# mLSTM start states padded with zero rows per pair of heads, and the low part of the differential queries in both row halves: products over all 128 rows

## The chip, the core and the metric

The kernel runs on one core of one Trainium2 chip. A core has a matrix engine (TensorE, PE in the profile, with its weight loads as PEld), a vector engine (VectorE, DVE), a scalar engine (ScalarE, ACT), GpSimd (POOL) and a synchronisation engine (SyncE, SP) that only issues transfers here. The metric is the device time of one execution in microseconds; 0.5% is 8.5 us.

## The reference, cut to what matters

One inference step of two layers over 640 tokens: 512 latent tokens (tiles 0 to 3 of 128) and 128 context tokens (tile 4). Layer 0 has eight latent-attention heads and four differential heads, layer 1 an mLSTM of eight heads in two directions; a feed-forward block follows each. Two places matter.

A differential head subtracts two attention maps, each with 64 features:

```python
k1, k2 = dk_all[..., :DIFF_HD], dk_all[..., DIFF_HD:]      # DIFF_HD = 64
p = softmax_probs(q1, k1, scale_b) - lam * softmax_probs(q2, k2, scale_b)
out = jnp.einsum('bhqk,bhkd->bhqd', p, dv_all)
```

An mLSTM head computes, per chunk of tokens and direction, a sum of two products: weighted scores times values, and queries times the state before the chunk (64 x 128, with a normaliser as column 129):

```python
s = jnp.einsum('bhcld,bhcsd->bhcls', qc, kc) * jnp.exp(dlog - m_t[..., None])
inter = jnp.exp(m_inter - m_t)
num = jnp.einsum('bhcls,bhcse->bhcle', s, vc) + inter[..., None] * jnp.einsum('bhcld,bhcde->bhcle', qc, Cp)
den = jnp.sum(s, axis=-1) + inter * jnp.einsum('bhcld,bhcd->bhcl', qc, np_)
```

## The kernel before

Activations stay in the core's memory; weights are streamed. SyncE loads a weight tile `wr` (L170) into a ring of four buffers, ScalarE rounds it to a high part `whi` (L180) and VectorE subtracts to get the low part `wlo` (L181). A product with weights is three products: high by high, high by low, low by high (L275 to L277, L295). The same ring of four also holds differential query stacks `qst`, mLSTM keys by token `kn` and, in layer 1, the tiles `state`. The instructions of an engine run in the order of its program; an engine that waits holds up all that is behind it.

*Differential heads* (about 262 to 340 us). `q_stack(t, p)` makes the queries of token tile t for a pair of heads: for each of two maps ScalarE writes the high part into both row halves (L897, L898), and GpSimd writes the low part (L899) into the 64 rows of that map only, both maps into the same 128 columns. The keys `kst` hold a map's high part in one row half and its low part in the other. A map's score (L947, L948) is then a product over 128 rows with the high queries (512 latent columns, then 128 cached ones), and a second over 64 rows with the low queries. Maximum and exponential (VectorE L859, ScalarE L864), combination, transposes (L873) and value products (L975) follow, in a software pipeline in which other items' products stand between.

*The mLSTM loop* (about 1057 to 1163 us) takes ten steps. A table, `HEAD_STEP`, sets the order of the parts in a step and which head each is for; the heads overlap, so that the outputs of one head run beside the scores of the next. Heads come in pairs: the even one has its 64 features in rows 0 to 63, the odd one in rows 64 to 127 (`rows_of(h)`, short `rr`). The parts that matter:

- `load_pair` (L1284): per pair, the tile `state`, the queries `qp` times a decay (broadcast by SyncE L1288, product on GpSimd L1291).
- `s_mm` (L1363): scores `st`, five products over the 64 rows of the head.
- `s_mul` (L1370, L1372): VectorE multiplies by the decays `D`, GpSimd masks.
- `s_state` (L1394, L1400): six products `cs` give a chunk's contribution; VectorE updates the states before chunks 2 to 4 of both directions, on the head's 64 rows. The state before the first chunk is the given one, `C0n`, loaded once (L1162).
- `last_state` (L1407): products `cst` for the final states of the context tokens.
- `o_mm` (L1422, L1423): for a token tile and a direction, the state product over the head's 64 rows, then the value product over 128 rows into the same sums `ho`. In the rows, `ho<-ph,qp` is a state product with the given state, `ho<-state,qp` one with an updated state.
- `o_post` (L1429 to L1437): ScalarE and VectorE divide by the normaliser and add the two directions; `h_norm` (L1453 to L1461) norms the head.

In steps 6 to 8 the table `LOOP_OUT` puts transposes (`mt`, L397) and first output products (`op`, L275 to L277) between the parts.

Of the kernel before, what the change touches and what calls it, by code (L numbers as in the profile page):

```python
# [17 lines left out]
NT = 5            # token tiles of 128: 0-3 latent (sample), 4 context (prompt)  # L18
# [6 lines left out]
# adaLN dots of later vectors (pairs of half dots), spread over the steps of the phases  # L25
ADA_IN = [0, 0, 0, 2, 2, 2, 2, 2, 1, 1, 1, 0, 0]     # by product of the input projections
ADA_FFN = [0] + [2] * 8 + [1] * 13                   # by feed-forward tile of layer 0
ADA_VO = [1, 0, 1, 1]                                # by column chunk of layer 1's values and output gates
ADA_MLA = {1: 1, 2: 1, 3: 1, 4: 1, 5: 1, 6: 1, 9: 1, 11: 1, 13: 1, 14: 1, 16: 1, 19: 1, 21: 1, 24: 2, 26: 1, 28: 1, 29: 1, 31: 1, 33: 1, 34: 1, 36: 1, 38: 1}     # half dots beside an item of MLA (head * 5 + tile)
# attention pipeline: order of the parts within a step, and how many items behind the newest a part is  # L30
# [4 lines left out]
# key stacks (head, map) beside an item of MLA  # L35
KEY_STACKS = {2: [(0, 0), (0, 1), (1, 0)], 10: [(1, 1)], 11: [(2, 0)], 15: [(2, 1), (3, 0)], 17: [(3, 1)], 16: [(4, 0)], 26: [(4, 1)]}
# transposes of a finished half tile (tile, half) after the differential item (tile, head)
MERGED_T = {(3, 3): [(2, 1), (4, 1)], (2, 2): [(1, 1)], (1, 3): [(0, 0), (0, 1)], (2, 0): [(1, 0)], (3, 2): [(2, 0), (3, 0), (4, 0)]}
# what follows the attention: first halves and rest of the output products, by tile
ATT_END = [('begin', 0), ('begin', 2), ('begin', 1), ('step', 4), ('step', 1), ('begin', 3), ('step', 2), ('T', 3), ('step', 0), ('step', 3)]  # L40
# a step of the mLSTM loop: its parts, and their head's distance from the step
HEAD_STEP = [('last', -2), ('state', -1), ('scores', 0), ('out0', -1), ('keys', 0), ('weights', 0), ('out1', -1), ('out3', -1), ('pair', 1), ('out2', -1), ('out4', -1), ('decay', 1)]
# work of the output projection that is taken into the loop, before a part of a step
LOOP_OUT = {(7, 'scores'): [('begin', 0)], (6, 'out3'): [('T', 2)], (7, 'out1'): [('T', 3)], (8, 'out0'): [('T', 4)], (8, 'weights'): [('begin', 1)], (6, 'keys'): [('T', 0)], (6, 'out4'): [('T', 1)], (8, 'out2'): [('begin', 2)], (8, 'decay'): [('begin', 3)]}
OUT_ORDER = [4, 0, 2, 1, 3]
GROUPS = [(0, 8), (8, 16), (16, 22)]   # feed-forward tiles of 128 by group
# [8 lines left out]
def _build(ctx, tc, nc, A):  # L55
# [6 lines left out]
    sp = pool("sp", 12)  # L62
# [37 lines left out]
    # ------------------------------------------------------------ constants  # L100
# [14 lines left out]
    def sigmoid(out, src):  # L115
        # 1 / (1 + exp(-src)) = exp(-ln(1 + exp(-src)))
        S.activation(out, src, AF.Exp, scale=-1.0)
        S.activation(out, out, AF.Ln, bias=ones[0:out.shape[0]])
        S.activation(out, out, AF.Exp, scale=-1.0)

    # silu(c): columns for the tensor engine, and rows on all partitions for the vector engine
# [9 lines left out]
    # ------------------------------------------------------------ weights: streamed, split in two  # L131
# [63 lines left out]
    def done(n=1, prep=True):  # L195
        # without prep the next weights are loaded, and split by a later call
# [8 lines left out]
    # ------------------------------------------------------------ adaLN  # L205
# [8 lines left out]
    def ada_dot(l, j, m, w, cs_=(0, 1)):  # L214
        # w [128 features, 1024]: products with silu(c), summed along the row
# [57 lines left out]
    # ------------------------------------------------------------ products  # L273
# [5 lines left out]
    def nat(ps, hh, hl, t, ch, part=None):  # L279
        # ps [128 tok, cols] = h[tile t] @ w chunk; a part: only the first or second half of the sum  # L280
# [9 lines left out]
    def trans_gemm(outs, wh, wl, hh, hl, nkc=8):  # L290
        # outs: [(psum ap, column slice)]; psum = w^T @ h^T[:, columns]
# [11 lines left out]
    def start_pair(us, wfs, hh, hl, norm_last):  # L303
        # the first two products after a norm leave the last token tiles for the end: their norm comes last
# [5 lines left out]
    # ------------------------------------------------------------ norms  # L310
# [8 lines left out]
    @contextmanager  # L319
    def after_split():  # L320
        # what the block traces is issued behind the last split
        with tc.issue_after(split_ins[0]), tc.issue_after(split_ins[1]):
            yield
# [7 lines left out]
    def ssq0(x_ap):  # L331
        # mean square of the first half of the columns, plus eps
# [49 lines left out]
    class Halves:  # L382
        # h^T of a mixer's output, high and low part of a column half in one tile
# [119 lines left out]
    o = 0  # L503
# [1152 lines left out]
```

## Time and profile before

| | |
|---|---|
| median of three runs | 1692.18 us (1684.17 to 1692.19) |
| span of the profiled execution | 1689.8 us (its own time is about 2.4 us more) |
| TensorE busy | 1662.4 us, 98% of the span |
| VectorE, ScalarE, GpSimd busy | 975.3 us, 697.5 us, 143.2 us |
| differential heads, 262 to 340 us | TensorE 75.58, VectorE 62.76, ScalarE 66.96, GpSimd 17.85 us |
| mLSTM loop, 1056.6 to 1163 us | TensorE 105.89, VectorE 74.98, ScalarE 56.09, GpSimd 43.02 us |

The shares of the whole span hide the stages: the feed-forward blocks take some 1000 of the 1690 us and are dense products. The two last lines of the table are windows on the two stages that the change touches. A TensorE record's printed length holds the pipeline's fill, so consecutive records overlap; how long one really takes is read from the distance between starts.

### The profile page before, as it was taken

Reading aid. Unit: us, or ns where it says so; the run is one execution under the profiler, and the core shown is the slowest. Engines: PE = TensorE matmul, PEld = TensorE weight load, DVE = VectorE, ACT = ScalarE, POOL = GpSimd, SP = SyncE. Lnnn points to the kernel's source line nnn. Section 1 sums busy time; section 2 is a strip of 40 time slices with the busy share of each in tenths; the row PEclk is TensorE's granted clock in tenths of the full one; section 3 lists DMA queues with packets and bytes.
Section 4 is the critical chain, followed back from the end, with each engine's and each line's share of the span. In section 5 each row is a group of like instructions: output and inputs, shape, how many; then the busy total and the mean of one; then the engine's idle time right before and its main releaser. Section 6 shows DMA issues by size and latency. Waiting matters only on the chain.

```text
span 1689.8 us, 24496 instructions
## 1 busy us (share of the span) xinstructions
PE 1662.4 (98%) x9704; PEld 1495.6 (89%) x9704; DVE 975.3 (58%) x1714; ACT 697.5 (41%) x1462; POOL 143.2 (8%) x171
## 2 busy tenths in 40 slices
PE   8999999999999999999999999999999999999998
PEld 7878888788998899889989979777899989998996
DVE  7788887856665655445475385856643343334335
ACT  5433568836332233223262256644643213322332
POOL 0001101210000000000010015532100000000000
PEclk8999999999999999999999999969999999999999
DMA  9363130052453433233225335323332122213211
GB/s 337 121 198 123 51 101 1 14 177 75 147 174 103 147 125 112 67 108 113 88 100 175 125 120 187 99 63 118 107 115 74 56 92 83 75 51 100 76 38 63
DMA packets 55970, 181.55 MB, mean 107 GB/s; under 512 B 7120, under 2 KB 9936, under 8 KB 55856
## 3 DMA queue, kind: packets, MB, share of 16 engines
q1 hardware_dynamic: 51152, 165.07, 30.5%
q0 software_dynamic: 4560, 14.73, 2.6%
q8 instruction: 76, 1.25, 0.3%
q14 instruction: 38, 0.31, 0.1%
q10 hardware_dynamic: 144, 0.20, 0.0%
HBM read 173.26 MB, written 6.71 MB: 106 GB/s over the span
## 4 chain that ended last, share of the span: by engine, by line
PE 93%; DVE 3%; ACT 3%; DMA 1%; issue 0%; SPq 0%; POOL 0%; DVEq 0%; ACTq 0%
PE ffa L295 18%; PE ffb L295 18%; PE fo L277 6%; PE fo L275 6%; PE fo L276 6%; PE qk L295 3%; PE op L275 2%; PE op L277 2%; PE op L276 2%; PE in L275 2%; PE av L931 2%; PE in L277 2%; PE in L276 2%; PE vo L277 2%; PE s L915 2%; PE vo L276 2%
## 5 line engine op out<-in xcount | busy, mean ns | idle before, releaser
L180 ACT CAST whi<-wr 128x1024 fp32r<-128x1024 f32 (+2 forms) x195 | 200.9, 1033 | 621.9 <-PE ffa L295 210.9
L181 DVE TENSOR_TENSOR wlo<-wr,whi 128x1024 fp32r<-128x1024 f32 (+2 forms) x195 | 236.0, 1214 | 222.6 <-ACT whi L180 221.1
L218 DVE SCALAR_TENSOR_TENSOR junk<-araw,cB 128x1024 bf16<-128x1024 f32 x160 | 195.1, 1247 | 32.3 <-DMA araw<-w_adaT 31.9
L277 PE MATMUL fo<-whi,hl 128*128 128x512 f32 (+1 forms) x446 | 175.6, 394 | 0.0
L275 PE MATMUL fo<-whi,hh 128*128 128x512 f32 (+1 forms) x446 | 174.7, 392 | 0.0
L276 PE MATMUL fo<-wlo,hh 128*128 128x512 f32 (+1 forms) x446 | 173.9, 390 | 0.0
L295 PE MATMUL ffa<-hl,whi 128*128 128x320 f32 (+1 forms) x704 | 164.2, 311 | 0.0
L295 PE MATMUL ffa<-hh,whi 128*128 128x320 f32 (+1 forms) x704 | 163.7, 310 | 0.0
L295 PE MATMUL ffa<-hh,wlo 128*128 128x320 f32 (+1 forms) x704 | 162.8, 309 | 0.0
L295 PE MATMUL ffb<-hl,whi 128*128 128x320 f32 (+1 forms) x704 | 162.1, 308 | 0.7 <-DVE hl L328 0.7
L295 PE MATMUL ffb<-hh,whi 128*128 128x320 f32 (+1 forms) x704 | 162.0, 308 | 0.3 <-ACT hh L327 0.2
L295 PE MATMUL ffb<-hh,wlo 128*128 128x320 f32 (+1 forms) x704 | 160.9, 306 | 0.0
L295 PEld LDWEIGHTS ffb<-hl,whi 128*128 128x128 f32 x704 | 118.2, 187 | 1.1 <-DVE hl L328 1.1
L295 PEld LDWEIGHTS ffb<-hh,whi 128*128 128x128 f32 x704 | 118.1, 188 | 0.9 <-ACT hh L327 0.9
L295 PEld LDWEIGHTS ffb<-hh,wlo 128*128 128x128 f32 x704 | 118.7, 188 | 0.0
L295 PEld LDWEIGHTS ffa<-hh,wlo 128*128 128x128 f32 x704 | 118.7, 188 | 0.0
L295 PEld LDWEIGHTS ffa<-hh,whi 128*128 128x128 f32 x704 | 118.2, 188 | 0.5
L295 PEld LDWEIGHTS ffa<-hl,whi 128*128 128x128 f32 x704 | 118.3, 187 | 0.1
L403 DVE TENSOR_TENSOR tmp<-fo,g 128x512 f32<-128x512 f32 (+1 forms) x61 | 41.6, 681 | 131.8 <-PE fo L277 131.7
L276 PEld LDWEIGHTS fo<-wlo,hh 128*128 128x128 f32 x446 | 83.8, 188 | 19.7
L277 PEld LDWEIGHTS fo<-whi,hl 128*128 128x128 f32 x446 | 83.8, 188 | 18.9
L275 PEld LDWEIGHTS fo<-whi,hh 128*128 128x128 f32 x446 | 83.7, 188 | 18.5
(362 smaller groups left out, 3047.6 us busy)
## 6 DMA issues: line engine op xcount, KB each, us to landing
wr<-ffi SPq DMA_DIRECT2D x88, 512.0 KB, 3.7
araw<-w_adaT SPq DMA_DIRECT2D x80, 512.0 KB, 4.1
wr<-ffo SPq DMA_DIRECT2D x44, 512.0 KB, 3.5
D<-m_dram SPq DMA_DIRECT2D x16, 320.0 KB, 4.2
ada<-w_ada SPq DMA_DIRECT2D x9, 512.0 KB, 9.7
wr<-winvo SPq DMA_DIRECT2D x12, 384.0 KB, 3.3
wr<-w_oab SPq DMA_DIRECT2D x8, 512.0 KB, 4.0
g<-gd POOLq DMA_DIRECT2D x8, 512.0 KB, 6.3
```

The source lines that it names most:

```text
L180: S.copy(hi, raw)
L181: V.tensor_tensor(out=lo, in0=raw, in1=hi.bitcast(F32), op=ALU.subtract)
L218: V.scalar_tensor_tensor(out=junk, in0=w, scalar=1.0, in1=cB[:, c, :], op0=ALU.mult, op1=ALU.mult, accum_out=vecs[l][:, j, m, c:c + 1])
L275: PE.matmul(ps, sh, mh, start=first, stop=False)
L276: PE.matmul(ps, sh, ml, start=False, stop=False)
L277: PE.matmul(ps, sl, mh, start=False, stop=last)
L295: PE.matmul(ps, w_(kc), h_[:, kc, sl], start=(kc == 0 and i == 0), stop=(kc == nkc - 1 and i == 2))
L403: V.tensor_tensor(out=tmp, in0=ps, in1=gate[:, 0 if t < 4 else 1, cols], op=ALU.mult)
L915: PE.matmul(sps[:, p, 0:320], qa[0:96, tok], ka[0:96, p * 320:(p + 1) * 320], start=True, stop=True)
L931: PE.matmul(ops[:, 0:64], st["PT"][:, b * 128:(b + 1) * 128], vhead[h][:, kb + b, :], start=(b == 0), stop=(b == nb - 1))
```

## The change

1. `q_stack` writes the low queries of each map into both row halves, in 128 columns for each map (the tile grows from 384 to 512 columns a head). GpSimd makes four subtractions a stack instead of two. The low score products then contract all 128 rows, as the high ones do.
2. The updated states live in a tile of their own, `stp`, zeroed once by GpSimd at the start, with a slot for each head of a pair; a slot holds the head's state in its 64 rows and zeros in the other head's rows. `o_mm` multiplies all 128 rows of `qp` with such a slot. The number of products, their columns and VectorE's updates (64 rows) stay. The tile `state` no longer takes a buffer of the weight ring.
3. The given states come padded with zero rows from the host (`C0p`): two transfers instead of one at the start of layer 1, and one more, issued by GpSimd, in `load_pair` for the third and fourth pair.
4. To make room: eleven instead of twelve buffers in the pool of small tiles, and a smaller room (4096 bytes) for the descriptors of transfers that GpSimd issues. Comments are stripped, so line numbers shift.

```diff
-    sp = pool("sp", 12)
+    sp = pool("sp", 11)
+    stp = cp.tile([128, 2, 2, 2, 3, 129], F32, name="stp")
+    G.memset(stp.rearrange("p a e d k c -> p (a e d k c)"), 0.0)
...
     def q_stack(t, p):
-        q_ = qst[(t, p)] = Wp.tile([128, 2, 384], F32R, name=nm("qst"), tag="raw", bufs=4)
+        q_ = qst[(t, p)] = Wp.tile([128, 2, 512], F32R, name=nm("qst"), tag="raw", bufs=4)
         for i in range(2):
             src = dqT[own(i), 2 * p:2 * p + 2, t * 128:(t + 1) * 128]
-            S.copy(q_[own(i), :, i * 128:(i + 1) * 128], src)
-            S.copy(q_[other(i), :, i * 128:(i + 1) * 128], src)
-            G.tensor_tensor(out=q_[own(i), :, 256:384], in0=src,
-                            in1=q_[own(i), :, i * 128:(i + 1) * 128].bitcast(F32), op=ALU.subtract)
+            hi = slice(i * 128, (i + 1) * 128)
+            S.copy(q_[own(i), :, hi], src)
+            S.copy(q_[other(i), :, hi], src)
+            for r in (own(i), other(i)):
+                G.tensor_tensor(out=q_[r, :, 256 + i * 128:384 + i * 128], in0=src, in1=q_[own(i), :, hi].bitcast(F32), op=ALU.subtract)
...
-                for w, rr in ((q_[:, i * 128:(i + 1) * 128], slice(0, 128)), (q_[r, 256:384], r)):
-                    PE.matmul(sps[:, 0, :], w, kst[h][rr, i, :], start=(w.shape[0] == 128), stop=(w.shape[0] == 64))
-                    PE.matmul(sps[:, 1, 0:128], w, kst[4][rr, h, i, :], start=(w.shape[0] == 128), stop=(w.shape[0] == 64))
+                for part in range(2):
+                    w = q_[:, part * 256 + i * 128:part * 256 + (i + 1) * 128]
+                    PE.matmul(sps[:, 0, :], w, kst[h][:, i, :], start=(part == 0), stop=(part == 1))
+                    PE.matmul(sps[:, 1, 0:128], w, kst[4][:, h, i, :], start=(part == 0), stop=(part == 1))
...
-    C0n = carve(1032).rearrange("p (d a c) -> p d a c", d=2, c=129)
+    C0p = carve(1032).rearrange("p (a e d c) -> p a e d c", a=2, e=2, c=129)
...
-    G.dma_start(C0n, A["C0n"])
+    for a in range(2):
+        G.dma_start(C0p[:, a], A["C0p"][a])
...
     def load_pair(pr):
-        states[pr] = Wp.tile([128, 2, 3, 129], F32, name=nm("state"), tag="raw", bufs=4)
+        states[pr] = stp[:, pr % 2]
+        if pr > 1:
+            G.dma_start(C0p[:, pr % 2], A["C0p"][pr])
...
     def s_state(h):
-                before = states[pr][rr, d, k - 1, :] if k else C0n[rr, d, pr, :]
-                V.scalar_tensor_tensor(out=states[pr][rr, d, k, :], in0=before, scalar=decs[pr][rr, d, i:i + 1],
+                before = states[pr][rr, h % 2, d, k - 1, :] if k else C0p[rr, pr % 2, h % 2, d, :]
+                V.scalar_tensor_tensor(out=states[pr][rr, h % 2, d, k, :], in0=before, scalar=decs[pr][rr, d, i:i + 1],
...
     def o_mm(h, t):
-                before = states[pr][rr, d, k - 1, :] if k else C0n[rr, d, pr, :]
-                PE.matmul(pv[:, d, :], qp_of(pr, d)[rr, t * 128:(t + 1) * 128], before, start=True, stop=False)
+                before = states[pr][:, h % 2, d, k - 1, :] if k else C0p[:, pr % 2, h % 2, d, :]
+                PE.matmul(pv[:, d, :], qp_of(pr, d)[:, t * 128:(t + 1) * 128], before, start=True, stop=False)
...
-    nc = bacc.Bacc("TRN2", target_bir_lowering=False, num_devices=1)
+    nc = bacc.Bacc("TRN2", target_bir_lowering=False, num_devices=1, dynamic_dma_scratch_size=4096)
```

On TensorE, in the loop, the outputs of one head (its token tiles 0, 3 and 1) before, where `D` are the masked scores and `state`, `ph` the updated and the given state:

```order
L1422 MATMUL ho_10264<-ph_8147,qp_9551 128x129
L1423 MATMUL ho_10264<-v_1640_8682,D_10103 128x129
L1422 MATMUL ho_10284<-state_10057,qp_9551 128x129
L1423 MATMUL ho_10284<-v_1640_8682,D_10103 128x129
L1422 MATMUL ho_10284<-state_10057,qp_9551 128x129
L1423 MATMUL ho_10284<-v_1640_8682,D_10110 128x129
L1422 MATMUL ho_10297<-state_10057,qp_9551 128x129
L1423 MATMUL ho_10297<-v_1640_8682,D_10103 128x129
L1422 MATMUL ho_10264<-state_10057,qp_9551 128x129
L1423 MATMUL ho_10264<-v_1640_8682,D_10110 128x129
```

and after:

```order
L1431 MATMUL ho_10281<-ph_8165,qp_9570 128x129
L1432 MATMUL ho_10281<-v_1640_8701,D_10120 128x129
L1431 MATMUL ho_10301<-stp,qp_9570 128x129
L1432 MATMUL ho_10301<-v_1640_8701,D_10120 128x129
L1431 MATMUL ho_10301<-stp,qp_9570 128x129
L1432 MATMUL ho_10301<-v_1640_8701,D_10127 128x129
L1431 MATMUL ho_10314<-stp,qp_9570 128x129
L1431 MATMUL ho_10281<-stp,qp_9570 128x129
L1432 MATMUL ho_10281<-v_1640_8701,D_10127 128x129
L1432 MATMUL ho_10314<-v_1640_8701,D_10120 128x129
```

The products stand in the same alternation, but for one value product that now comes two places later; what differs is that L1431 reads 128 rows where L1422 read 64, which these rows don't print.

On SyncE, at the end of the loop, the last loads of decays (`D`, of the last heads) and of output weights (`w_oc`) before:

```order
L1305 DMA D_10363<-m_dram 128x640 [waits DMAHW4_49,PE_49,Pool_49]
L170 DMA wr_10507<-w_oc 128x1024 [waits DMAHW5_49,DVE_49]
L1305 DMA D_10493<-m_dram 128x640 [waits DMAHW6_49,PE_49,Pool_49]
L1411 DMA o_C<-co_10373 64x2x128 [waits DMAHW7_49,Activation_49]
L1305 DMA D_10500<-m_dram 128x640 [waits DMAHW0_49,PE_49,Pool_49]
L170 DMA wr_10941<-w_oc 128x1024 [waits DMAHW1_49,DVE_49,PE_49]
L1411 DMA o_C<-co_10516 64x2x128 [waits DMAHW2_49,Activation_49]
L170 DMA wr_10947<-w_oc 128x1024 [waits DMAHW5_49,DMAHW3_49,DVE_49]
```

and after:

```order
L1313 DMA D_10380<-m_dram 128x640 [waits DMAHW4_49,PE_49,Pool_49]
L173 DMA wr_10524<-w_oc 128x1024 [waits DMAHW5_49]
L173 DMA wr_10958<-w_oc 128x1024 [waits DMAHW6_49,DVE_49]
L173 DMA wr_10964<-w_oc 128x1024 [waits DMAHW7_49,Pool_49]
L1419 DMA o_C<-co_10390 64x2x128 [waits DMAHW0_49,Activation_49]
L1313 DMA D_10510<-m_dram 128x640 [waits DMAHW1_49,PE_49]
L1313 DMA D_10517<-m_dram 128x640 [waits DMAHW2_49,PE_49]
```

Two loads of output weights now stand ahead of the last head's decays, one of them behind a wait for GpSimd.

On GpSimd, in the differential heads, two query stacks in a row before:

```order
L899 TENSOR_TENSOR qst_2988<-Sa_662,qst_2988 64x2x128 x2
L899 TENSOR_TENSOR qst_3159<-Sa_662,qst_3159 64x2x128 x2
L992 TENSOR_TENSOR mg_1385<-mg_1385,rq_2852 128x512
L993 TENSOR_TENSOR mg_1385<-mg_1385,ph_135 128x512
L899 TENSOR_TENSOR qst_3266<-Sa_662,qst_3266 64x2x128 x2
```

and after:

```order
L904 TENSOR_TENSOR qst_2996<-Sa_664,qst_2996 64x2x128 x4
L904 TENSOR_TENSOR qst_3169<-Sa_664,qst_3169 64x2x128 x4
L997 TENSOR_TENSOR mg_1387<-mg_1387,rq_2858 128x512
L998 TENSOR_TENSOR mg_1387<-mg_1387,ph_137 128x512
L904 TENSOR_TENSOR qst_3278<-Sa_664,qst_3278 64x2x128 x4
```

Each stack's group has four operations in place of two; the norm of a finished tile (`mg`) stays behind the same stack.

## Rows read from the trace of the kernel before

**Rows 1.** The page: span, busy time of the engines, chain that ended last.

```profile
span 1689.8 us, 24496 instructions
...
PE 1662.4 (98%) x9704; PEld 1495.6 (89%) x9704; DVE 975.3 (58%) x1714; ACT 697.5 (41%) x1462; POOL 143.2 (8%) x171
...
PE 93%; DVE 3%; ACT 3%; DMA 1%; issue 0%; SPq 0%; POOL 0%; DVEq 0%; ACTq 0%
```

**Rows 2.** Time line of TensorE in the loop (start, length, instruction, shape, count).

```profile
1090.90 0.37 PE L1422 MATMUL ho<-ph,qp 64*128 64x129 f32 x1
1091.01 0.27 PE L1363 MATMUL st<-qk 64*128 64x128 f32 x1
...
1091.43 0.49 PE L1423 MATMUL ho<-v,D 128*128 128x129 f32 x2
1091.85 0.49 PE L1422 MATMUL ho<-state,qp 64*128 64x129 f32 x2
1092.27 0.49 PE L1423 MATMUL ho<-v,D 128*128 128x129 f32 x2
...
1093.52 0.71 PE L1422 MATMUL ho<-state,qp 64*128 64x129 f32 x4
1094.16 0.71 PE L1423 MATMUL ho<-v,D 128*128 128x129 f32 x4
```

**Rows 3.** The same time line after the clock has fallen.

```profile
1111.44 2.84 PE L1394 MATMUL cs<-v,ph 128*64 128x129 f32 x12
1114.21 1.22 PE L1363 MATMUL st<-qk 64*128 64x128 f32 x4
...
1120.72 0.80 PE L1422 MATMUL ho<-state,qp 64*128 64x129 f32 x2
1121.45 0.80 PE L1423 MATMUL ho<-v,D 128*128 128x129 f32 x2
```

**Rows 4.** Windows by loop step: stretch, length, busy of each engine (records), clock.

```profile
1067.89:1076.55 8.66, 8.66 (x59) 6.78 (x59) 7.33 (x22) 5.75 (x22) 5.08 (x6) 1.00 0.45 109
1076.55:1087.43 10.88, 10.88 (x68) 8.35 (x67) 10.36 (x35) 7.33 (x31) 7.88 (x10) 1.00 0.33 90
...
1097.31:1111.44 14.13, 13.62 (x69) 10.09 (x68) 11.15 (x34) 8.09 (x34) 8.09 (x11) 0.82 0.39 108
1111.44:1125.94 14.50, 14.50 (x56) 11.36 (x55) 5.59 (x17) 5.71 (x24) 2.06 (x3) 0.50 0.16 51
...
sum 105.12, PE 104.61 PEld 79.74 DVE 74.00 ACT 54.81 POOL 42.99; mean PE 11.62 PEld 8.86 DVE 8.22 ACT 6.09 POOL 4.78
```

**Rows 5.** Time line of TensorE before the fall: idle time and its releaser in brackets.

```profile
1103.52 0.49 PE L1422 MATMUL ho<-state,qp 64*128 64x129 f32 x2 [0.49 <-DVE state L1400]
```

**Rows 6.** Windows of 2 us where the clock falls and where it returns.

```profile
1106.00:1108.00 2.00, 2.00 (x10) 1.66 (x9) 1.18 (x7) 0.95 (x6) 1.58 (x3) 0.56 0.63 248
...
1136.00:1138.00 2.00, 2.00 (x9) 1.65 (x8) 1.49 (x6) 1.44 (x6) 0.00 (x0) 0.76 0.66 242
```

**Rows 7.** Time line of TensorE in the differential heads.

```profile
293.46 0.48 PE L947 MATMUL s<-kst,qst 128*128 128x512 f32 x1
...
293.93 0.49 PE L947 MATMUL s<-kst,qst 64*128 64x512 f32 x1
...
294.42 0.50 PE L947 MATMUL s<-kst,qst 128*128 128x512 f32 x1
...
300.78 0.50 PE L947 MATMUL s<-kst,qst 128*128 128x512 f32 x1
...
301.18 1.12 PE L975 MATMUL av<-Sb,ph 128*128 128x128 f32 x8
```

**Rows 8.** Windows of 20 us, 260 to 340 us: one, and the sum.

```profile
300.00:320.00 20.00, 19.07 (x121) 14.46 (x120) 18.06 (x44) 18.20 (x57) 5.38 (x7) 1.00 0.00 1
...
sum 80.00, PE 77.58 PEld 60.52 DVE 63.68 ACT 68.47 POOL 17.85; mean PE 19.39 PEld 15.13 DVE 15.92 ACT 17.12 POOL 4.46
```

**Rows 9.** Time line of GpSimd: the second subtraction of a query stack.

```profile
286.23 0.73 POOL L899 TENSOR_TENSOR qst<-Sa,qst 64x256 fp32r<-64x256 f32 x1 [1.28 <-ACT qst L897]
```

More of the change, by code (lines that the diff above doesn't have):

```diff
@@ L1414, in o_mm @@
     def o_mm(h, t):
-        pr, rr = h // 2, rows_of(h)
+        pr = h // 2
         po = u1("ho")
@@ L1616, in _layout @@
     C0 = np.concatenate([f("state_mlstm_C")[0, 0], f("state_mlstm_n")[0, 0][..., None]], -1)
-    d["C0n"] = C0.reshape(2, 4, 2, 64, 129).transpose(2, 3, 0, 1, 4).reshape(128, 2, 4, 129)
+    C0 = C0.reshape(2, 4, 2, 64, 129)
+    C0p = np.zeros((4, 2, 64, 2, 2, 129), np.float32)
+    for e in range(2):
+        C0p[:, e, :, e] = C0[:, :, e].transpose(1, 2, 0, 3)
+    d["C0p"] = C0p.reshape(4, 128, 2, 2, 129)
     m0 = f("state_mlstm_m")[0, 0]
```

## The prediction

> **What bounds the kernel now.** I read the page first: the profiled execution has a span of 1689.8 us, TensorE is busy 98% of it and holds 93% of the chain that ended last [rows 1]. The reported times of the three runs are 1692.18, 1684.17 and 1692.19 us; what lies around the span is about 2.4 us (1692.2 less 1689.8), so the profiled execution is one like the median, and I count from 1692.2. A TensorE that is always busy says little by itself, because a busy record may be waiting for its weights. So the second view is the time line of TensorE in the two stages that the change touches: the mLSTM loop (about 1057 to 1163 us) and the differential heads (about 262 to 340 us). What to look for there is the distance from one start to the next, not the printed length of a record.
>
> In the loop, products over 64 rows (state products, L1422) alternate with products over 128 rows (values, L1423). Two records of one shape followed by two of the other take 0.42 us: 1091.43 to 1091.85, and 1091.85 to 1092.27. Four records of one shape take 0.64 us (1093.52 to 1094.16) [rows 2]. Two more of the same shape therefore cost 0.22 us, 0.11 each, and the two that came with a change of shape paid 0.42 less 0.22 = 0.20 us for it. At the lower of the two clock levels the same arithmetic holds: twelve records of one shape take 2.77 us (0.23 each, 1111.44 to 1114.21), an alternating pair 0.73 us (1120.72 to 1121.45), so 0.73 less 0.46 = 0.27 us a change [rows 3].
>
> The third view is the table of the loop by steps, cut at the products of the new states [rows 4]. TensorE fills each step, VectorE is at 7.33 of 8.66 and 10.36 of 10.88 us in two of them, and over 105.12 us VectorE is busy 74.00, ScalarE 54.81, GpSimd 42.99. VectorE is next in line, and close. The fourth is the clock: after a wait of 0.49 us of a state product for VectorE [rows 5], in a step with fewer records for its length than the ones before (69 in 14.13 us against 68 in 10.88) [rows 4], the granted clock goes to the lower level (1.2 GHz) and returns only when the dense products of the output projection run; the 2 us windows show 0.56 at 1106 and 0.76 at 1136, so some 30 us at half clock [rows 6].
>
> **The change part by part.** *State products over 128 rows.* Records and columns stay the same (128 state products); only the row shape changes. From the program order of both kernels I counted neighbours of different shape in the loop's TensorE program: 146 before, 46 after. So 100 changes go, at 0.20 us: 20 us of TensorE's 104.61. That a 128-row record is no dearer than a 64-row one by itself is in [rows 2]: 0.22 us for two of either, once the change is taken off. Without those changes and at full clock (half of 30 us, 15 us, comes back), TensorE would need 104.6 - 20 - 15 = about 70 us. It then isn't the bound: VectorE's 74.00 us are. How full VectorE can be is between its two fullest steps: 95% (10.36 of 10.88) gives 78 us for the loop, 85% (7.33 of 8.66) gives 87 [rows 4]. I take 84, nearer to the second, since VectorE there waits in chains (absolute value, maximum, reciprocal, scale) for ScalarE: 105 - 84 = **21 us saved**, bounds 18 to 27.
>
> The Trainium skill, TensorEngine Tiling (Performance Considerations, When to Use Tiling), speaks against this edit: a contraction of 64 should be run as two row tiles beside each other, not padded. The trace has such pairs, but few: a state product of one head starts at 1090.90 and a score product of the next head, in the other row half, 0.11 us later, within the state product's printed 0.37 us [rows 2]. By that rule alone each of the 64 pairs of state products could halve, 64 x 0.11 = 7 us (an estimate by that page), and the change would give it away; but the program puts no two state products of different halves together.
>
> What is lost of overlap is about two records in each of seven steps: 14 x 0.11 = **1.5 us added** (0 to 4.5, if each of them pays a change, 14 x 0.20, besides) [rows 2].
>
> *Low part of the differential scores over 128 rows.* A map's score is a pair of products (512 and 128 columns) over 128 rows, and a pair over 64. Pair to pair takes 0.47 us (293.46 to 293.93) and 0.49 (to 294.42). The one pair that stands between 128-row neighbours takes 0.40 (300.78 to 301.18) [rows 7]. 64 pairs at 0.08 are 5 us; at the loop's 0.20 a change they would be 13. But here ScalarE is nearly full: 18.20 of 20 us between 300 and 320, 68.47 of 80 over the stage [rows 8]. At 91% throughout the 80 us can't shrink below 75.2. So **4 us saved**, 0 to 5. The clock is 1.00 here throughout and gives nothing back.
>
> *More work on GpSimd.* A query stack takes four subtractions instead of two: 16 more at 0.73 us, 12 us of GpSimd. The last of a stack ends at 286.96 and its first low product starts at 293.93, 7 us later [rows 9, 7]; two more end at 288.4 and still come in time. That cover hides all of it. If VectorE were held up for as long as GpSimd works, it would cost 12 us of a stage in which VectorE is free for 16 of 80 [rows 8]; I count **1 us**, 0 to 4.
>
> *Edits with one answer, nothing:* the zeroing at the start (GpSimd, nothing is queued behind it there but a key load that is used in the differential heads), the start states in two transfers instead of one at the same place, and two more transfers issued by GpSimd in the loop, each a step ahead of its first reader; queued behind each is a masking operation on GpSimd, which is busy 42.99 of 105 us [rows 4]. One buffer less among the small tiles and less room for descriptors show in no wait of the loop. On SyncE's queue the states no longer occupy a buffer of the weight ring, so two loads of output weights move ahead of the last decay load (second piece of order in the section on the change); one of them waits for GpSimd's last reader of the keys. The decay is used a step later, and a step is 8.7 us or more [rows 4], so I add nothing; if that cover goes, it costs one transfer once.
>
> Sum: -21 - 4 + 1.5 + 1 = -22.5 us; 1692.2 - 22.5 = 1669.7, **1670 us**.
>
> **The rivals.** *The clock still falls for some 30 us* (1676). For it: VectorE will make TensorE wait more often than the one 0.49 us of now, and the fall came behind such a wait [rows 5, 6]. Against it: every step gets more records into its time, since the alternation was what stretched them. TensorE then needs 104.6 - 20 = 85 us, with waits about 90, so 15 instead of 21: 1692.2 - 15 - 4 + 2.5 = 1676.
>
> *The clock falls early and stays* (1713): the one that ends slower. If the waits for VectorE bring the lower level already in the second step, and it lasts until the output products, seven of nine steps run at half clock: 70 us x 7/9 = 54, doubled 109, and 18 for the last two, 127 instead of 105: +22 - 4 + 2.5 gives 1712.7. It decides the sign when the time at half clock is over twice the present 30 us (each further us there costs about half of one, and 22 are to be lost). For it speaks that TensorE would have 70 us of work in 84; against it that in the differential heads TensorE waits too (19.07 busy of 20) at a clock of 1.00 [rows 8].
>
> *It doesn't do what it says* (1694): the 0.42 us belong to the alternation of two products that add to one bank, not to the row shape; then only the additions are left, 1692.2 + 2.5 = 1694.7. Against it: in the four-and-four stretch, products into the same banks run at 0.16 each over the four [rows 2], and the pair between 128-row neighbours is quicker [rows 7].
>
> **How the numbers follow.** The forecast (clock holds, VectorE next) has a chance of 0.70, the 30 us fall 0.15, no effect 0.09, early fall 0.06. The forecast's bounds are -27 - 5 = -32 (1660) and -18 + 4.5 + 4 = -9.5 (1683); with the second case (1676) up to 1684 some 8 in 10 is covered: 1660 to 1684. A measurement here can tell 0.5%, 8.5 us, from no change, so faster means under 1683.7: 0.84 (the first two, less a little of their upper tail), same 0.10, slower 0.06.
>
> **What would show it.** Right: state and value products one behind the other at 0.11 us; 0.32 to 0.40 us a pair in the differential scores; a granted clock of 1.00 through the loop; waits of TensorE for VectorE's state updates that are not there now; the loop at 78 to 87 us and the differential stage 0 to 5 us shorter. Wrong: 0.42 us for two and two with all rows alike (the price isn't the shape); a clock of 0.50 in the loop (a rival); waits of the low score products for GpSimd (the cover is gone); or a loop of over 90 us at full clock, in which a chain through VectorE and ScalarE, and not VectorE's sum, sets the step.

## The result

The changed kernel takes 1663.07 us (median of four runs, 1662.57 to 1663.80) against 1692.06 us for the kernel before beside it (1684.17 to 1692.19); the ratio is 0.9856, with a 95% interval from 0.9818 to 0.9894. The profiled execution has a span of 1661.2 us instead of 1689.8. In later runs the kernel before lay between 1676 and 1692 us, with mean clocks over the whole execution from 0.997 to 0.985, and the execution profiled before the prediction was one at the slow end.

The page of the changed kernel, lines answering to [rows 1]:

```profile
span 1661.2 us, 24515 instructions
...
PE 1627.4 (98%) x9704; PEld 1483.4 (89%) x9704; DVE 975.0 (59%) x1714; ACT 693.5 (42%) x1462; POOL 162.2 (10%) x191
...
PE 90%; DVE 5%; ACT 3%; DMA 1%; issue 1%; POOL 0%; SPq 0%; DVEq 0%; ACTq 0%
```

TensorE has 35 us less of busy time, as many records as before, and VectorE's share of the chain has grown from 3% to 5%. The landmarks of the time line (first differential score, first output product, first score product of the loop, last value product) split the 28.6 us: 1.7 before the differential heads (the mean clock up to there was 0.97 and is 0.98), 4.3 in them (73.7 to 69.4 us), 23.0 in the loop (107.2 to 84.2), and 0.4 given back elsewhere.

The time line of TensorE in the loop, to set beside [rows 2] (start, length, instruction, shape, count):

```profile
1055.55 0.39 PE L1431 MATMUL ho<-stp,qp 128*128 128x129 f32 x2
1055.77 0.39 PE L1432 MATMUL ho<-v,D 128*128 128x129 f32 x2
1055.99 0.61 PE L1431 MATMUL ho<-stp,qp 128*128 128x129 f32 x4
1056.44 0.61 PE L1432 MATMUL ho<-v,D 128*128 128x129 f32 x4
1056.89 0.39 PE L1431 MATMUL ho<-stp,qp 128*128 128x129 f32 x2
1057.11 0.39 PE L1432 MATMUL ho<-v,D 128*128 128x129 f32 x2
```

State and value products alternate as they did, but two records take 0.22 us where they took 0.42. The reading order for the rest is that of [rows 4]: the whole loop in one window, before and after (stretch, length, busy of each engine with its records, mean clock):

```profile
1056.60:1163.80 107.20, 106.69 (x563) 81.58 (x563) 74.98 (x227) 56.20 (x232) 43.28 (x54) 0.86 0.26 75
```

```profile
1050.70:1134.90 84.20, 79.66 (x564) 70.56 (x564) 74.80 (x226) 54.36 (x230) 45.55 (x56) 0.94 0.36 102
```

TensorE's busy time falls by 27 us, VectorE's not at all, and VectorE is now busy 74.80 of 84.20 us, 89%. The clock is better (0.94 against 0.86) but not at 1.00. In the loop it falls twice, and each time TensorE has just waited for VectorE to empty a buffer of the sums:

```profile
1070.34 0.71 PE L1432 MATMUL ho<-v,D 128*128 128x129 f32 x4 [1.86 <-DVE hs L1446]
...
1091.36 0.71 PE L1432 MATMUL ho<-v,D 128*128 128x129 f32 x4 [2.13 <-DVE hs L1446]
```

The 2 us windows behind the second wait, and where the clock is coming back, show it as [rows 6] did:

```profile
1092.00:1094.00 2.00, 2.00 (x10) 1.66 (x10) 1.93 (x7) 2.00 (x11) 1.34 (x1) 0.56 0.34 120
1098.00:1100.00 2.00, 2.00 (x16) 2.00 (x15) 1.06 (x4) 1.18 (x7) 1.92 (x2) 0.74 0.90 220
```

In the differential heads, the pairs (512 and 128 columns) that [rows 7] had 0.47 to 0.49 us apart are 0.39 (290.69 to 291.08) and 0.35 us apart (291.08 to the value products at 291.43):

```profile
290.69 0.50 PE L952 MATMUL s<-kst,qst 128*128 128x512 f32 x1 [0.34 <-ACT P L867]
291.03 0.22 PE L953 MATMUL s<-kst,qst 128*128 128x128 f32 x1
291.08 0.45 PE L952 MATMUL s<-kst,qst 128*128 128x512 f32 x1
291.37 0.22 PE L953 MATMUL s<-kst,qst 128*128 128x128 f32 x1
291.43 1.11 PE L980 MATMUL av<-Sb,ph 128*128 128x128 f32 x8
```

TensorE has 7.1 us less to do there (71.28 to 64.20), the stage is only 4.3 us shorter; before, then after:

```profile
266.30:340.00 73.70, 71.28 (x451) 54.86 (x450) 59.38 (x150) 63.45 (x194) 16.40 (x18) 1.00 0.03 8
```

```profile
264.60:334.00 69.40, 64.20 (x451) 54.65 (x450) 60.63 (x150) 62.09 (x194) 28.25 (x32) 1.00 0.03 9
```

### The profile page after: what moved, and what is told of

It reads as the page before. It is cut to its first block, busy times and chain, and to the rows that moved or that the text cites. A ratio compares the mean times of both kernels' runs of the same rounds, so it can differ in the third digit from the quotient of the medians.

```text
span 1661.2 us, 24515 instructions
## 1 busy us (share of the span) xinstructions
PE 1627.4 (98%) x9704; PEld 1483.4 (89%) x9704; DVE 975.0 (59%) x1714; ACT 693.5 (42%) x1462; POOL 162.2 (10%) x191
## 4 chain that ended last, share of the span: by engine, by line
PE 90%; DVE 5%; ACT 3%; DMA 1%; issue 1%; POOL 0%; SPq 0%; DVEq 0%; ACTq 0%
PE ffa L298 19%; PE ffb L298 18%; PE fo L280 6%; PE fo L278 6%; PE fo L279 6%; PE qk L298 3%; PE in L278 2%; PE in L280 2%; PE op L278 2%; PE in L279 2%; PE op L280 2%; PE op L279 2%; PE vo L280 2%; PE s L919 2%; PE vo L279 2%; PE vo L278 2%
## 5 line engine op out<-in xcount | busy, mean ns | idle before, releaser
L184 DVE TENSOR_TENSOR wlo<-wr,whi 128x1024 fp32r<-128x1024 f32 (+2 forms) x195 | 235.3, 1210 | 225.3 <-ACT whi L183 223.5
```

The lines of the kernel that those rows point to most:

```text
L184: V.tensor_tensor(out=lo, in0=raw, in1=hi.bitcast(F32), op=ALU.subtract)
```

## The experiments

For each I give the loop's length, its mean clock, and their product: what the loop would take at full clock if TensorE alone set it. Where TensorE also waits for others, a low clock costs less than the product takes off, and the loop at full clock is longer than the product. Changes of shape are neighbours of different rows or columns among the loop's recorded products: 146 before, 46 after.

### The two parts apart

The first keeps the padded states and puts the differential scores back; the second is the kernel before with the differential part alone.

> The changed kernel with the differential scores put back (low products over 64 rows, two subtractions a query stack); the padded states stay. Shape theory (a change of row shape costs TensorE 0.20 us and lets the clock fall): the loop, from the first score product to the last value product, takes 84 us instead of 107, the differential stage (first score to first output product) 73 to 74 as before; in all 23 to 25 us below the kernel before, 1667 to 1669. Rival (the two parts need each other): less than 18 us below.

> The kernel before with the differential part of the change alone: low queries in both row halves, low products over 128 rows. Shape theory with ScalarE as next limit: the differential stage goes from 73.7 to 69 to 70 us, the loop stays at 107, in all 4 to 5 us below the kernel before, 1687 to 1688. Rival (GpSimd's 16 added subtractions hold up VectorE): differential stage 73 us or more, in all no gain.

Padded states alone: 1666.89 us (1666.10 to 1671.43), ratio 0.9906 (0.9875 to 0.9938); differential stage 73.6 us, loop 86.9 at a clock of 0.90, 78 at full clock. Differential part alone: 1676.31 us (1673.99 to 1688.03), ratio 0.9957 (0.9927 to 0.9987); differential stage 69.4 us, loop 98.0 at a clock of 0.95. The stages came out nearly as expected, each part in its own place (the loop of the first 3 us longer). The first lies only 15.7 us below the kernel before beside it (1682.59), which the expectation gave to its rival; but the expectation counted from 1692. The two ratios multiply to 0.9863, against 0.9856 for the whole change, so the parts don't need each other. That the loop of the second was 98.0 and not 107 was not expected: nothing in the loop differs from the kernel before, only the clock does.

```profile
1049.80:1147.80 98.00, 97.49 (x563) 74.89 (x563) 74.05 (x227) 55.90 (x232) 43.28 (x54) 0.95 0.26 82
```

98.0 x 0.95 = 93 and 107.2 x 0.86 = 92: the same loop program, in which TensorE is busy almost throughout, with the clock low for some 10 us in one and some 30 in the other. So part of the 23 us is the clock's, and varies from run to run.

### Everything but the rows

```diff
-        pr = h // 2
+        pr, rr = h // 2, rows_of(h)
...
-                PE.matmul(pv[:, d, :], qp_of(pr, d)[:, t * 128:(t + 1) * 128], before, start=True, stop=False)
+                PE.matmul(pv[:, d, :], qp_of(pr, d)[rr, t * 128:(t + 1) * 128], before, start=True, stop=False)
```

(and `rr` for the rows of `before`.)

> The changed kernel, but the state products contract only the head's own 64 rows of the padded tiles; the states' own tile, the ring without them, the moved loads and the differential part stay. Shape theory: the loop is back at 104 to 108 us with a long stretch at the lower clock, two records of one shape after two of the other 0.42 us apart, in all only the differential part's 4 to 6 us below the kernel before, 1686 to 1688. Rival (the gain comes from the ring and the moved loads): loop 84 to 90 us, 1663 to 1670.

1685.37 us (1677.71 to 1692.48), ratio 1.0012 (0.9981 to 1.0042). The states' own tile, the ring without them, the moved weight loads are all there, and the loop is long again, if less than expected (102.2 us; the clock was low for 17 us of it, not 30):

```profile
1051.10:1153.30 102.20, 100.81 (x565) 77.56 (x564) 75.28 (x227) 56.44 (x232) 44.49 (x56) 0.92 0.27 84
```

```profile
1091.83 0.49 PE L1431 MATMUL ho<-stp,qp 64*128 64x129 f32 x2
1092.24 0.49 PE L1432 MATMUL ho<-v,D 128*128 128x129 f32 x2
1092.66 0.49 PE L1431 MATMUL ho<-stp,qp 64*128 64x129 f32 x2
```

0.42 us again. The tiles and the ring are those of the changed kernel, so the rival falls: the edit to the row count is what separates 102.2 x 0.92 = 94 us from 84.2 x 0.94 = 79. The order of TensorE's products is not the same, though: by their starts, the loop's records come in the order of the kernel before, one for one, and 98 of some 565 stand elsewhere in the changed kernel. The next kernel shows the rows without that order.

### Half of the changes, two ways

One lets only the even heads have 128 rows (`rr = rows_of(h) if h % 2 else slice(0, 128)`). The other pads nothing and reorders the kernel before, so that one tile is state, value, value, state.

```diff
         for d in range(2):
             k = t if d == 0 else 3 - t
+            value = lambda first: PE.matmul(pv[:, d, :], PTs[(h, d)][:, t, :], v1[:, t, h, :], start=first or t == 4, stop=not first or t == 4)
+            if t == 4 or d == 1:
+                value(True)
...
-            PE.matmul(pv[:, d, :], PTs[(h, d)][:, t, :], v1[:, t, h, :], start=(t == 4), stop=True)
+                if d == 0:
+                    value(False)
```

> The changed kernel, with state products over 128 rows for the even heads only and over their 64 rows for the odd ones: half of the shape changes come back, some 95 in the loop instead of 46 or 146. If each costs its share: loop at full clock 86 to 87 us, between 79 and 94, and with some 10 us at the lower clock 91 to 92 us, 1669 to 1672. If the first half already frees TensorE as far as VectorE allows: loop 84 to 87, 1663 to 1666.

> The kernel before, no padding: in each latent token tile the backward direction's value product goes ahead of its state product, so that the order is state, value, value, state instead of state, value, state, value, and the next tile begins with the shape that the last one ended on. The work is the same. Shape theory: about half of the 129 changes of row count in the loop go, 55 to 65 at 0.15 to 0.20 us, 8 to 13 us of the loop at full clock (some 95 to 82 to 87 us), and the clock falls for 10 us or less; in all 1668 to 1674. Rival (the price belongs to the second product of a sum waiting for the first, not to the shape): loop unchanged within 3 us.

Even heads only: 1664.71 us (1662.89 to 1664.99), 95 changes, and

```profile
1050.30:1136.70 86.40, 84.28 (x563) 69.08 (x563) 74.70 (x227) 55.82 (x232) 44.45 (x56) 1.00 0.34 99
```

86.4 us at full clock, with TensorE's records in the order of the kernel with all rows at 64 but for 8 of them: these 6 to 8 us are the rows' alone. That is (94 - 86.4) / 51 = 0.15 us for each change taken away from the kernel with all rows at 64, or 0.11 from the 92 of the kernel before. For the rest (86.4 - 79) / 49 would be 0.15 again, but the 79 is a product of a loop in which TensorE waits, and so the most that they can be worth. Both expectations allow 86.4. The total lies in the range of the second, in which the first half frees TensorE almost as far as VectorE allows: it is 1.6 us above that of the full change. The clock did not fall in this one.

The reordering missed: 1677.87 us (1676.56 to 1686.64), ratio 0.9955 (0.9929 to 0.9980), and the loop 95.1 x 0.95 = 90 us. The order written down was not the order that ran: single state and value products still alternate in the trace, and only 21 changes went, not 60. That the loop hardly moved was what its rival foresaw, but with so few changes gone it doesn't speak for it. Its 90 us lie where 125 changes at 0.15 would put them (94 less 3), but a difference of 3 us is about what such a loop varies; it doesn't show the rule by itself.

### More work, a better clock

```diff
+                PE.matmul(pv[:, d, :], PTs[(h, d)][:, t, :], v1[:, t, h, :], start=True, stop=True)
                 PE.matmul(pv[:, d, :], qp_of(pr, d)[rr, t * 128:(t + 1) * 128], before, start=True, stop=False)
```

> The kernel before, with the value product of the four latent tiles run once more ahead of each state product and overwritten by it: 64 products of two records more, 14 us of TensorE at 0.22 each, over 128 rows and without another change of shape. If what TensorE has to do between the changes keeps the clock up: no long stretch at the lower level, the loop at 106 to 109 us as before in spite of 14 us more work. If the clock falls all the same: 14 us and what of them falls into the slow stretch more, loop 122 to 130 us, 1706 to 1715.

1691.77 us (1690.22 to 1692.93), ratio 1.0040 (1.0018 to 1.0061).

```profile
1053.20:1162.60 109.40, 108.95 (x693) 87.38 (x692) 73.43 (x227) 58.34 (x232) 43.31 (x54) 1.00 0.26 74
```

With 128 records more (and 156 changes of shape, ten more than meant), the loop takes 2.2 us longer than in the profiled kernel before: the clock stays at its upper level throughout. In all ten runs the mean clock of the whole execution was 0.995 to 0.997; the 26 runs of the kernel before beside them had 0.985 to 0.995, and their median, 1682.59, is 9 us lower. 109.4 less 14 is 95 us, so the kernel before at full clock needs about 92 to 95. That bounds the clock's share of the profiled 23 us: 107.2 x 0.14 = 15 us lost to it before, and after 84.2 x 0.06 = 5 at most, since TensorE waits in that loop anyway. So 10 to 15 of the 23 are the clock's, and 8 to 13 the shape's.

### GpSimd's added subtractions alone

> The kernel before with the four subtractions a query stack (the larger stack too), but the low score products still over the map's own 64 rows: GpSimd's added 12 us without the new shape. If the cover that the prediction named holds: differential stage 73 to 74.5 us as before, no wait of a low product for GpSimd over 0.5 us. If GpSimd's work holds up VectorE: stage 75 us or more.

1691.80 us (1679.38 to 1698.34), ratio 1.0009 (0.9974 to 1.0043). The differential stage takes 74.0 us, 0.3 more than before, with GpSimd at 28.25 us instead of 16.40:

```profile
266.40:340.40 74.00, 71.47 (x452) 54.99 (x450) 60.72 (x150) 63.39 (x194) 28.25 (x32) 1.00 0.03 8
```

VectorE's busy time rises by 1.3 us (from 59.38); the longest wait of a weight load for a subtraction was 0.2 us. The cover holds.

### What bounds the two stages now

Five kernels start from the changed one. The first moves the norm of the fifth tile from VectorE to GpSimd (`n = NT`). The second pads the keys of the scores too, the third copies the second half of a query stack by transfers, and the last two join these, one with the norm moved (the second diff has the form that it takes there):

```diff
+    def pad_keys(h):
+        rr = rows_of(h)
+        SP.dma_start(kz[rr, h % 2, :], kT[rr, h // 2, :])
...
-            PE.matmul(flat(st)[:, tok], kT[rr, pr, tok], qT[rr, pr, tok], start=True, stop=True)
+            PE.matmul(flat(st)[:, tok], kz[:, h % 2, tok], qT[:, pr, tok], start=True, stop=True)
```

```diff
-            S.copy(q_[other(i), :, hi], src)
-            for r in (own(i), other(i)):
-                G.tensor_tensor(out=q_[r, :, 256 + i * 128:384 + i * 128], in0=src, in1=q_[own(i), :, hi].bitcast(F32), op=ALU.subtract)
+            G.tensor_tensor(out=q_[own(i), :, 256 + i * 128:384 + i * 128], in0=src, in1=q_[own(i), :, hi].bitcast(F32), op=ALU.subtract)
+            half = lambda r: q_[r].rearrange("p a (l i c) -> p (a l) i c", l=2, c=128)[:, :, i, :].bitcast(F32)
+            SP.dma_start(half(other(i)), half(own(i)))
```

> The changed kernel with the fifth token tile's head norm moved from VectorE to GpSimd for seven heads (0.8 us each on VectorE, 5.7 us of its 74.8 in the loop of 84.2). If VectorE's sum sets the loop now, as the prediction said: loop 78 to 80 us, 1657 to 1659. If it is chains through VectorE, ScalarE and the buffers of the sums: 82 to 85 us, 1661 to 1664. If GpSimd's longer operation delays masks: over 85.

> The changed kernel, with the score products of the loop over 128 rows too: each head's keys are copied by a transfer into a tile with zeros in the other head's rows (one slot for even, one for odd heads; the updated states keep one slot a parity to make room). If TensorE's remaining 25 changes of row count still bound the loop: 25 x 0.15 = 4 us less in the loop, 80 us, 1659. If the chain through VectorE and the buffers of the sums bounds it: loop 83 to 85 us, 1662 to 1664.

> The changed kernel, with the second row half of each query stack (high and low part) copied by a transfer instead of by ScalarE and GpSimd: ScalarE loses 16 casts of 0.4 us, 6.5 us, in the differential heads, GpSimd 12 us. If ScalarE is what bounds that stage now: stage 69.4 to 66 us, 1660. If TensorE is (72.7 busy of 78 us) or the chain of one item: 68 to 70 us, no difference that can be told. If the transfer comes late: TensorE waits for it, over 70 us.

> The changed kernel with the padded keys and with the query stacks' second half copied by transfers, together. If the two gains stand in different stages and add: differential stage 66 us, loop 80 to 82, 1653 to 1655. If the gain of one was the clock's alone and the other's transfers or earlier start bring the fall back: 1658 or more.

> The kernel with padded keys and copied stacks, and the fifth tile's norm on GpSimd besides. TensorE is no longer full there (74.6 of 81.1 us with padded keys, VectorE 73.1). If VectorE's sum sets that loop: 5.7 us less of it, loop 76 to 78 us, 1649 to 1651. If chains: loop 80 to 82, 1653 to 1655.

*Norm on GpSimd*: 1662.82 us (1661.66 to 1665.46), no gain; loop 86.4 us at 0.94, in the range of the third expectation. The work left VectorE (seven operations, 5.4 us), the busy time didn't (75.62 us). About half of what came back is seen in one small operation of VectorE, the maximum of 128 x 2 elements in the normaliser. Its rows in the changed kernel and in this one (busy, mean ns of one), in the window from 1050 to 1164 us:

```profile
L1439 DVE TENSOR_TENSOR s<-s,ph 128x2 f32<-128x2 f32 x40 | 14.1, 374 | 3.0 <-ACT s L1438 2.8
```

```profile
L1439 DVE TENSOR_TENSOR s<-s,ph 128x2 f32<-128x2 f32 x40 | 16.9, 443 | 3.0 <-ACT s L1438 2.6
```

(1.9 us more came back in the weight subtractions, L184.) In the kernel before its mean was 277 ns. In the loops of these three kernels 45 of these operations are overlapped by no instruction of GpSimd, and none of the 45 took over 0.16 us; the other 69 have means of 0.42, 0.48 and 0.64 us. Four of these operations in the changed kernel stand where GpSimd works almost without a gap: the time line of VectorE first, then GpSimd's at the same time:

```profile
1085.66 2.01 DVE L1439 TENSOR_TENSOR s<-s,ph 128x2 f32<-128x2 f32 x1 [0.18 <-ACT s L1438]
...
1088.66 1.85 DVE L1439 TENSOR_TENSOR s<-s,ph 128x2 f32<-128x2 f32 x3
```

```profile
1085.87 0.77 POOL L1380 TENSOR_SCALAR_AFFINE_SELECT D<-D 128x640 f32<-128x640 f32 x1
1086.59 1.05 POOL L1466 TENSOR_TENSOR hs<-hs,hq 128x512 f32<-128x512 f32 x1
...
1089.24 1.26 POOL L1467 TENSOR_TENSOR hs<-hs,og 128x512 f32<-128x512 f32 x1
```

One operation on 256 elements takes 2.01 us and ends when GpSimd's two operations end (1087.64 us); three more end at 1090.51, with GpSimd's next at 1090.50. The wait of TensorE that precedes the second fall of the clock (2.13 us up to 1091.36, above) begins at 1089.23, while VectorE is held like this. With the norm on GpSimd one of three such operations took 4.15 us, and TensorE's longest wait follows (VectorE, then TensorE):

```profile
1084.57 4.29 DVE L1439 TENSOR_TENSOR s<-s,ph 128x2 f32<-128x2 f32 x3
```

```profile
1091.58 1.23 PE L1432 MATMUL ho<-v,D 128*128 128x129 f32 x4 [4.29 <-DVE hs L1446]
```

*Keys padded*: 1658.45 us (1657.79 to 1660.03). No change of row count is left, 32 of column count are, and the loop takes 81.1 us at a clock of 1.00:

```profile
1049.30:1130.40 81.10, 74.60 (x564) 66.26 (x563) 73.12 (x226) 54.84 (x230) 44.98 (x56) 1.00 0.44 124
```

That is nearer the first expectation (80 us, 1659) than the second, but TensorE is busy in only 74.60 us of it, so it isn't full. Whether the 3 us came from the rows or from a clock that didn't fall isn't told apart. *Copies by transfer*: 1658.41 us (1657.70 to 1662.02); the differential stage goes from 69.4 to 65.9 us, ScalarE's busy time there from 62.09 to 57.10:

```profile
265.80:331.70 65.90, 62.36 (x450) 54.32 (x449) 59.18 (x150) 57.10 (x181) 17.39 (x18) 1.00 0.16 37
```

The edit takes 11 us from GpSimd too. But TensorE's weight loads waited for ScalarE's exponentials (in all, times, longest wait, in us; the changed kernel, then this one) and in the changed kernel for GpSimd at most 0.3 us:

```profile
PEld s L952 <- ACT P L867: 7.0, 14, 1.1
```

```profile
PEld s L952 <- ACT P L867: 4.4, 11, 0.8
```

So ScalarE was the bound, as the prediction had it. *Both*: 1656.86 us (1655.97 to 1657.77), differential stage 66.0, loop 81.7 at 0.98; ratio to the kernel before 0.9860 (0.9841 to 0.9880). The gains don't add fully: 1663.1 less 4.6 less 4.7 would be 1653.8. *Both, with the norm on GpSimd*: 1657.04 us (1655.63 to 1658.35), loop 82.3, no gain again, and above both expectations (1649 to 1651, 1653 to 1655). The version with both is the fastest found, about 6 us below the changed kernel's 1663.07, which was not run beside it.

## Why the prediction was right, and where it wasn't

*The price of a change of shape* held: 0.42 us became 0.22. It was read off one time line as 0.20 us of TensorE. Three loops at a clock of 1.00 price it without the product: TensorE is busy 95 us with 156 changes (109 less 14), 84.3 with 95, 74.6 with 32, which is 0.17 and 0.15 a change. Of the loop's length the first half of the changes is worth 0.11 to 0.15 each, the second at most that. The rest of TensorE's gain went into waits: 0.5 us of them before, 4.6 after.

*A slip*: the records of state products are 128, but the products 64; a float32 product is recorded twice. The 100 changes were counted between products, so that the sum wasn't touched.

*The loop*, -21 forecast, -23.0 measured, inside 18 to 27; 84.2 us with VectorE 89% busy, where I took 84 and so 88%. The sum was right for a partly wrong reason, and in part by luck. I let the clock come back whole; a third of the time at the lower level stayed (10 of 31 us). And the 105 us that I counted from belong to an execution whose clock was low for 31 us: at full clock the loop before needs 92 to 95, and the same 84 would have been a gain of about 10.

*VectorE is next* was right as an address; that its sum is a fixed price was wrong. I priced the loop by that sum, as if work taken from it would shorten the loop. Moving 5.4 us to GpSimd gave nothing, twice; but VectorE's busy time didn't fall by it, so these runs don't tell what a smaller sum would give. They show that part of the sum is made by GpSimd: of VectorE's 74.8 us in the changed loop some 9 are that one small operation's wait (40 of them at 0.37 us instead of 0.16, an estimate from the rows above), and some 5 before. VectorE is late in the stretches where GpSimd is busy beside it, and TensorE waits behind those. The sign that I named, waits for the state updates, is not what came: the two long waits (1.86 and 2.13 us) are for the emptying of the sums (L1446). The Trainium skill, SBUF - State Buffer (Who interferes with whom), says that a VectorE instruction with two inputs in that memory contends with a GpSimd instruction that reads it, and that the lock on the ports they share is exclusive. The 2.01 us row agrees. My term for this, 1 us in the differential heads, had only looked at the other stage. That GpSimd's work is what stands behind the whole of the remaining loop time I have argued from those rows, not shown: no run took work from GpSimd in the loop.

*The differential stage*, -4 forecast, -4.3 measured, with ScalarE as the limit: the run that took 5 us from ScalarE gained 3.5, and TensorE's waits there are for ScalarE. TensorE's own saving was 7.1 us, not the 5 that I made of 0.08 us a pair; it didn't matter, because the limit held.

*GpSimd's subtractions* cost 0.3 us of the 0 to 4. *Lost overlap* of 64-row neighbours can't be told from the rest. *The edits at nothing* are bounded only loosely, by the kernel with 64 rows, which has nearly all of them and the differential part besides. Its loop at full clock, 94, lies among the 92 to 95 of the kernels without them. But its total shows nothing of the differential part's gain (ratio 1.0012, where that part alone has 0.9957); the traces put at most 2 us of this in the loop at full clock, and that the clock is the rest isn't shown.

*The rivals.* "It doesn't do what it says" falls with the kernel of 64 rows. The two on the clock were half right: the clock does fall after waits for VectorE, earlier than before (1071 and 1092 against 1106 us), but for some 10 us in all; it returns while the loop goes on, not only with the output products. So both had the duration wrong. That such a wait is the trigger, as they and I assumed, isn't shown. With the keys padded TensorE waits 1.91 us for VectorE, and the clock stays at 1.00 through that loop:

```profile
1068.84 0.71 PE L1438 MATMUL ho<-v,D 128*128 128x129 f32 x4 [1.91 <-DVE hs L1452]
```

With the subtractions alone it falls at 1106.6 us, and from the loop's start to there TensorE's only recorded waits are two, together 0.5 us (the waits, then the window of the fall):

```profile
PE ho L1427 <- DVE state L1405: 0.5, 2, 0.3
```

```profile
1106.00:1108.00 2.00, 2.00 (x9) 1.63 (x9) 1.29 (x4) 0.65 (x5) 1.91 (x3) 0.66 0.68 270
```

*The base.* The 1692 that I counted from was one of the kernel's longer times. In three later sets of runs its medians were 1680.6, 1682.6 and 1689.9, so that the change is worth 18 to 27 us by these, though the changed kernel was not run beside them. Runs with the same mean clock over the whole execution lie closer: at 0.991 the kernel before took 1680.0 to 1680.6 us and the changed one 1662.9 and 1663.8; at 0.995 to 0.997 it took 1676.0 to 1676.8, and the changed one, at 0.996, 1663.2. That is 17 and 13 us, about 4 of them in the differential heads. The kernel before moves with the clock; the changed one hardly does.

## What to carry to other kernels

Read the distance between starts, and look for it jumping where products of different row counts alternate: here each such neighbour cost TensorE 0.15 to 0.20 us, and zero rows, which add no time to a product (0.22 us for two records over 128 rows, as for two more of 64), remove it. The stage gains that only as far as the next engine lets it. When TensorE is the bound and the clock falls in that stage, price the shape and the clock apart and compare with more than one execution before. Before taking work from the engine that is next in line, see whether its small operations are long: an engine that is held by another isn't helped by giving that other one more to do.

## What the runs showed of the hardware that I had not expected

Adding work can cost less than its own time when the clock stays up with it: 14 us of products made the loop 2.2 us longer than in the execution profiled before (a clock of 1.00 instead of 0.86), and the median of the runs 9 us longer. The same loop program took 98 us in one execution and 107 in another, by the clock alone. The Trainium skill, TensorEngine Tiling (Key Properties), says that a change of tiling mode drains TensorE, without a price. The runs put a price on the change between 64 and 128 rows, 0.15 to 0.20 us at the upper clock level; that it is a drain none of them shows. A VectorE operation on 256 elements, 0.16 us undisturbed, can take 2.01 and 4.15 us beside GpSimd.
